# Two gate-and-query projections of layer 1 as seven quarter products each, and a schedule that books the port shared by VectorE and GpSimd

## The chip, the cores and the metric

The kernel runs on one core of a Trainium2 chip. The metric is the time of one launch in microseconds on the device; three runs are given, and one further execution was taken by the hardware profiler.

## The reference, cut to what matters

Two layers on x of 512 tokens x 1024 channels in float32. Layer 0 is a mix of an mLSTM and a sparse attention; layer 1, which the change touches, is a gated linear recurrence with 8 heads of 128:

```python
def hgrn2_layer(h, w_in, b_in, lb, head_norm, w_out):
    proj = h @ w_in + b_in                    # h: 512 x 1024, w_in: 1024 x 4096
    fp, iv, qp, z = jnp.split(proj, 4, axis=-1)
    logf = jnp.log(lb + (1.0 - lb) * jax.nn.sigmoid(fp))
    k = (1.0 - lb) * jax.nn.sigmoid(-fp)
    q = jax.nn.silu(qp)
    o = hgrn2_chunkwise(heads(q), heads(k), heads(iv), heads(logf))
    o = rms_norm(o, head_norm)
    return (o * jax.nn.silu(z)) @ w_out

x = x + layer(rms_norm(x, norm_w))            # for both layers
```

## The kernel before

Every float32 product is made of three float32r products. `cvt_w` splits a weight block of 128 x 1024 into a high part (two ScalarE copies of 512 columns, `whi<-raw`) and a low part (one VectorE subtraction, `wlo<-raw,whi`); activations are split likewise (`h1h`, `h1l`). A matmul triple is then high x high, high weight x low activation, low weight x high activation. Weights come as 512 KB loads on SyncE's queue into 3 buffers `raw` and are split into 4 buffers `whi`, `wlo`, each as soon as the block before in that buffer has been used.

Layer 1's input projection is cut by pairs of heads. `t0` to `t3` give gate and query of two heads each (512 columns: gate and query of one head, then of the other), `r0` to `r3` value and output gate. The order is t0, p0, t1, t2, t3, p1, then the output projections o10 and o11. p0 and p1 are `Pair`: two r projections made at once by Strassen's method, seven products instead of eight, from weight sums in DRAM (`wt`) and activation sums `S1` to `S4` (tiles `ss`). A t projection is a `Group`: 4 blocks of 128 columns, 8 blocks of 128 rows, 3 products, each a matmul that streams 512 tokens past a 128 x 128 weight: 96 matmuls. Its result for a block lies in a PSUM bank (`mx` or `my`); `t_evac` multiplies it by the tokens' norm `rsB` on VectorE and makes from a gate `f` and the key `HB[:, 2]`, from a query `HB[:, 0]` and `HB[:, 1]`.

The recurrence of a head, `hgrn(h)`, takes 7 levels of small matmuls (`sd`, `tq`) and VectorE products on `HB`, then a tail that needs the head's values from p0 or p1. It starts once both heads of a t projection are there, and runs among the next projections' matmuls: heads 0 and 1 in p0, 2 and 3 in t2, 4 and 5 in t3, 6 and 7 in p1, with tails later.

The weight sums are made in layer 0 by GpSimd's own DMA queue from DRAM to DRAM (`AQ.put`): `sums(q, n)` issues step n of eight for pair q, four copies, two accumulations from the weights, and the two steps `t2 += t3` and `t4 += t2` (`wt<-wt`), one step in each of the eight groups nkv to o00, at fixed places of the group's order.

The order of all instructions on every engine is worked out at build time. Generators (`Flow`) emit work in an order of priority; then `Plan.schedule` is a list schedule in which each operation has a price (`price`), begins when its operands, its engine and its buffers are free, and the one with the earliest due time goes first. Six rounds are made and the best by its own clock is kept. Only the order of instructions goes into the program; on the chip each engine runs its own in that order and waits for semaphores. One engine's begin looks at its own clock alone:

```python
def begin(o):
    if o.eng != "T":
        return max(clock[o.eng], o.ready)
```

All instructions have the line of a helper (L407), so rows are told apart by tile names, buffer numbers left out.

Of the kernel before, what the change touches and what calls it, by code (L numbers as in the profile page):

```python
# [28 lines left out]
HBN = 4  # L29
# [7 lines left out]
def _r(a, n):  # L37
# [121 lines left out]
class Op:  # L159
    __slots__ = ("eng", "fn", "a", "k", "cost", "acc", "pred", "succ", "left", "ready", "start", "end", "done", "late", "after",  # L160
                 "load", "cols", "idx", "first", "tiles", "tab", "next")


class Plan:
# [5 lines left out]
    def __init__(self):  # L170
        self.ops, self.hist, self.masks = [], {}, {}
        self.tag, self.order, self.bufs = {}, {}, {}
        self.clock = dict.fromkeys("TVAPQ", 600.0)
        self.xfer, self.table, self.cols = 0.0, 0, [0.0] * 4
        self.born = {}
# [26 lines left out]
    def add(self, eng, fn, a, k, cost):  # L202
# [6 lines left out]
        o.next = None  # L209
        aps = [(x, j == 0) for j, x in enumerate(a) if isinstance(x, bass.AP)]  # L210
# [72 lines left out]
    def schedule(self, pe):  # L283
# [8 lines left out]
        clock, xfer, table, cols = dict(self.clock), self.xfer, self.table, list(self.cols)  # L292

        def begin(o):
            if o.eng != "T":
                return max(clock[o.eng], o.ready)
# [43 lines left out]
        while n_left:  # L340
# [23 lines left out]
            x.end = x.done = clock[e] = t + cost  # L364
            if e == "T":
# [23 lines left out]
        return max(o.done for o in self.ops), (clock, xfer, table, cols)  # L389

    def flush(self, rounds, live=()):
# [10 lines left out]
        (_, (self.clock, self.xfer, self.table, self.cols), when) = best  # L402
# [113 lines left out]
def price(name, fn, a, k):  # L516
# [12 lines left out]
    if k.get("op") == OP.pow:  # L529
        return 300 + 165 * n  # L530
# [4 lines left out]
    return 150 + (2.1 if fn == "tensor_tensor" else 0.86) * n  # L535
# [5 lines left out]
class Paced:  # L541
# [5 lines left out]
    def __getattr__(self, fn):  # L547
        f = getattr(self.eng, fn)

        def go(*a, **k):  # L550
            aps = [x for x in a if isinstance(x, bass.AP)]
            ns = k.pop("_price", None) or price(self.name, fn, a, k)
# [4 lines left out]
            self.plan.add(self.name, f, a, k, ns)  # L557
# [57 lines left out]
def build(tc, I, out):  # L615
# [6 lines left out]
    with ExitStack() as ctx:  # L622
# [258 lines left out]

        def split(name):
# [10 lines left out]
        def rstd(accs, rs, rsB, ev, TPS=TPS, tp_t=tp_t):  # L893
# [7 lines left out]
            P.tensor_tensor(rs, rs, hm[:, :4], op=OP.pow, _price=1950.0)  # L901
# [20 lines left out]
        wt = [dp.tile([128, 8192], F32, name=f"wt{q}", tag=f"wt{q}") for q in range(2)]  # L922
        x1d = dp.tile([128, 8, 512], F32, name="x1d", tag="x1d")
# [5 lines left out]
        def sums(q, n):  # L929
# [4 lines left out]
                     (t1, wblock(b, 0), 1), (t3, wblock(b, 1), 1), (t2, t3, 1), (t4, t2, 1)]  # L934
            AQ.put(*steps[n])
# [10 lines left out]
        with ExitStack() as c0:  # L946
# [738 lines left out]
            def dense0():  # L1685
                for n_, g in enumerate(seq[:-1]):
# [25 lines left out]
        with ExitStack() as c1:  # L1712
# [242 lines left out]

            def t_evac(pr):
                def go(j4, p):
                    hh, j = divmod(j4, 2)
                    h = 2 * pr + hh
                    c = 4 * pr + j4  # L1960
                    t = w_t("tt")
                    V.tensor_tensor(t, p, rsB, op=OP.mult)
                    if j == 0:
                        hbr[0] -= 1
                        assert hbr[0] >= 0
                        HBs[h] = s_t("HB", [128, 3, 512], HBN)
                        fs[h] = s_t("f", [128, 512], HBN)
                        f = fs[h]
                        A.activation(f, t, AF.Sigmoid, bias=pcc("t", c))
                        sg = w_t("sg")  # L1970
                        A.activation(sg, t, AF.Sigmoid, scale=-1.0, bias=ntb[:, c:c + 1])
                        V.tensor_scalar(f, f, oml[:, h:h + 1], lb[:, h:h + 1], op0=OP.mult, op1=OP.add)
                        A.activation(HBs[h][:, 2, :], sg, AF.Copy, scale=oml[:, h:h + 1])
                    else:
                        HB = HBs[h]
                        sq = w_t("sgq")
                        A.activation(sq, t, AF.Sigmoid, bias=pcc("t", c))
                        V.scalar_tensor_tensor(HB[:, 0, :], t, pcc("t", c), sq, op0=OP.add, op1=OP.mult)
# [134 lines left out]
```

## Time and profile before

| | us |
|---|---|
| median of 3 runs | 624.26 |
| lowest and highest of them | 619.97, 624.37 |
| the profiled execution | 622.05 |
| its span, first to last instruction | 620.3 |
| TensorE busy | 610.5 (98%) |
| VectorE busy | 464.6 (75%) |
| ScalarE busy | 326.6 (53%) |
| GpSimd busy | 106.0 (17%) |

PE is TensorE's matmul row, PEld its weight loads, DVE VectorE, ACT ScalarE, POOL GpSimd, SP SyncE; a q behind a name is the engine's queue of instructions that issue or wait. Matmuls overlap and their ends are modelled, so the spacing of their starts says more than their length. x96 behind a name counts instructions; "<-" in brackets names what ended the idle time before.

### The profile page before, as it was taken

The page shows a single profiled execution, that of the slowest core. Times are in us where ns is not written, and L with a number is a line of the kernel's source. Part 1 is how long each engine was busy: PE and PEld are TensorE (multiplying, and loading weights), DVE is VectorE, ACT ScalarE, POOL GpSimd, SP SyncE. Part 2 cuts the span into 40 slices and gives each one's busy share as a digit, 9 for nine tenths or more (in the row PEclk, how much of TensorE's full clock was granted, in tenths as well). Part 3 has the DMA queues.
Part 4 walks back from the last instruction along what each step waited for, and adds up shares of the span by engine and source line. Part 5 has one row for each costly group of instructions (what it writes and reads, how often), then busy time and mean ns, then how long its engine had stood idle before and what let it go on. Part 6 is the DMA issues. An engine that isn't in the chain of part 4 may idle for free.

```text
span 620.3 us, 11687 instructions
## 1 busy us (share of the span) xinstructions
PE 610.5 (98%) x4498; PEld 492.5 (79%) x4498; DVE 464.6 (75%) x979; ACT 326.6 (53%) x778; POOL 106.0 (17%) x140
## 2 busy tenths in 40 slices
PE   8999998999999999999999999999999999999997
PEld 8977886877777777888878887788877877788886
DVE  5878989979888775556555659997588798986441
ACT  6554433676666764373434657456427375565410
POOL 1224351110000010074103110113000100122100
PEclk9998999999999999999999999999999999999999
DMA  8733545625234028048964424374222215473111
GB/s 287 259 139 107 151 133 189 203 70 170 101 71 135 1 42 248 0 122 277 240 209 136 136 89 148 109 230 141 63 77 70 70 32 175 134 281 130 35 69 68
DMA packets 23526, 82.90 MB, mean 134 GB/s; under 512 B 3376, under 2 KB 4272, under 8 KB 20656
## 3 DMA queue, kind: packets, MB, share of 16 engines
q1 hardware_dynamic: 21168, 65.39, 31.9%
q0 software_dynamic: 2304, 16.78, 10.6%
q8 instruction: 35, 0.57, 0.4%
q14 instruction: 19, 0.16, 0.1%
HBM read 77.96 MB, written 20.97 MB: 159 GB/s over the span
## 4 chain that ended last, share of the span: by engine, by line
PE 86%; DVE 6%; DMA 3%; issue 1%; POOL 1%; ACT 1%; SPq 0%; ACTq 0%; DVEq 0%
PE mm L407 30%; PE mx L407 17%; PE my L407 15%; PE sc L407 7%; PE tp L407 5%; PE tq L407 5%; PE ac L407 4%; DMA raw<-in_wall_dram 3%; PE sd L407 2%; DVE wlo L407 1%; POOL krs L407 1%; DVE q L407 1%; DVE x L407 1%; DVE HB L407 1%; DVE ivgg L407 1%
## 5 line engine op out<-in xcount | busy, mean ns | idle before, releaser
L407 ACT ACTIVATE whi<-raw 128x512 fp32r<-128x512 f32 (+1 forms) x184 | 104.9, 614 | 74.7 <-PE my L407 29.3
L407 DVE TENSOR_TENSOR wlo<-raw,whi 128x1024 fp32r<-128x1024 f32 (+1 forms) x96 | 115.3, 1208 | 17.4 <-ACT whi L407 17.2
L407 PE MATMUL mm<-wlo,h0h 128*128 128x512 f32 (+1 forms) x168 | 68.1, 408 | 0.0
L407 PE MATMUL mm<-whi,h0h 128*128 128x512 f32 (+1 forms) x168 | 68.0, 407 | 0.0
L407 PE MATMUL mm<-whi,h0l 128*128 128x512 f32 (+1 forms) x168 | 67.6, 403 | 0.0
L407 ACT ACTIVATE PP<-sc,nm 128x128 f32<-128x128 f32 (+2 forms) x64 | 33.7, 527 | 22.8 <-DVE nm L407 19.4
L407 DVE CUSTOM_DVE_ANT_0 sc<-sc,cz 128x128 f32<-128x128 f32 (+2 forms) x64 | 31.5, 501 | 13.3 <-PE sc L407 10.2
L407 PE MATMUL mm<-h0l,whi 128*128 128x512 f32 x96 | 39.1, 407 | 0.0
L407 PE MATMUL mm<-h0h,whi 128*128 128x512 f32 x96 | 39.0, 406 | 0.1
L407 PE MATMUL mm<-h0h,wlo 128*128 128x512 f32 x96 | 38.1, 396 | 0.4 <-DVE wlo L407 0.4
L407 PEld LDWEIGHTS mm<-whi,h0l 128*128 128x128 f32 x168 | 32.2, 192 | 5.7
L407 PEld LDWEIGHTS mm<-wlo,h0h 128*128 128x128 f32 x168 | 32.2, 192 | 5.7 <-issue 0.2
L407 PEld LDWEIGHTS mm<-whi,h0h 128*128 128x128 f32 x168 | 32.2, 192 | 5.4 <-issue 0.2
L407 DVE TENSOR_TENSOR HB<-HB,tt 128x512 f32<-128x512 f32 x48 | 31.9, 686 | 4.5 <-PE sd L407 3.1
L407 PE MATMUL sc<-kd,q 128*128 128x128 f32 (+3 forms) x128 | 31.8, 333 | 0.0
L407 ACT ACTIVATE PT<-tp 128x384 f32<-128x384 f32 (+1 forms) x48 | 24.1, 526 | 11.0 <-PE tp L407 10.8
L407 POOL TENSOR_TENSOR ivgg<-ivgg,zz 128x256 f32<-128x256 f32 x16 | 17.7, 1106 | 66.0 <-ACT zz L407 66.0
L407 PE MATMUL tp<-cs,PP 128*128 128x128 f32 x160 | 26.7, 276 | 0.0
L407 PEld LDWEIGHTS sc<-kd,q 128*128 128x128 f32 x128 | 22.9, 192 | 4.4 <-ACT PT L407 0.8
L407 PE MATMUL my<-h1l,whi 128*128 128x512 f32 x64 | 25.8, 404 | 0.0
L407 PE MATMUL mx<-h1l,whi 128*128 128x512 f32 x64 | 25.8, 403 | 0.0
L407 PE MATMUL mx<-h1h,whi 128*128 128x512 f32 x64 | 25.7, 402 | 0.0
(374 smaller groups left out, 1535.7 us busy)
## 6 DMA issues: line engine op xcount, KB each, us to landing
raw<-in_wall_dram SPq DMA_DIRECT2D x76, 512.0 KB, 4.1
wt<-in_wall_dram POOLq DMA_DIRECT2D x12, 1024.0 KB, 5.5
raw<-wt SPq DMA_DIRECT2D x16, 512.0 KB, 3.8
wt<-wt POOLq DMA_DIRECT2D x4, 1024.0 KB, 12.6
bias<-in_brow_dram SPq DMA_DIRECT2D x9, 256.0 KB, 4.7
xt<-in_xt_dram SPq DMA_DIRECT2D x8, 256.0 KB, 5.9
w<-in_cw_dram SPq DMA_DIRECT2D x2, 1024.0 KB, 8.8
x<-in_xt_dram SPq DMA_DIRECT2D x2, 1024.0 KB, 9.6
```

Of the source, the lines that this page charges most:

```text
L407: o.fn(*o.a, **k)
```

## The change

Projections t1 and t2 become `Quad`s. Each is seen as a 2 x 2 product of quarters: output columns by head, tokens by halves of 256, rows by halves of 512. Seven products p, each of a 512 x 256 weight quarter (or sum of quarters) and 256 tokens: 2 column blocks x 4 row blocks x 3 split products, 24 matmuls of 256 columns, 168 in all. Products 0, 3, 4, 5 add up in one PSUM bank X, product 1 has a bank Y, 2 and 6 a second Y; the four outputs come from the banks as they stand after products 1, 4, 5 and 6 and from copies of X made by ScalarE after products 0, 3 and 4 (tiles `hold`), added by VectorE. The weights take seven blocks of 512 KB instead of four, each split by `cvt_w`. The weight sums (`wq`) are made in DRAM by `qsums`, eight steps of 512 KB for each of the two projections, issued at four places of a group's order (6, 28, 50, 72) where there were two (10, 60). The host lays the columns of t1 and t2 out by quarters, query ahead of gate. A head's recurrence is handed over after product 5 or 6.

In the list schedule an operation of VectorE or GpSimd may hold a port: all of GpSimd's but memsets (200 ns for a power, else its price), and VectorE's with two inputs in SBUF or plain copies and scalar products from SBUF to SBUF. Such an operation begins no earlier than the port is free. GpSimd's prices are set anew (345 ns + 165 per element for a power, 165 + 2.22 for a product), and the fixed 1950 ns for the power in `rstd` goes.

```diff
+FAST = "t1", "t2"
 G1 = []
 for _p in range(4):
-    G1.append((f"t{_p}", _r(256 * _p, 128) + _r(2048 + 256 * _p, 128)
-               + _r(256 * _p + 128, 128) + _r(2048 + 256 * _p + 128, 128)))
+    _b = [_r(256 * _p, 128), _r(2048 + 256 * _p, 128), _r(256 * _p + 128, 128), _r(2048 + 256 * _p + 128, 128)]
+    G1.append((f"t{_p}", sum([_b[_j ^ (f"t{_p}" in FAST)] for _j in range(4)], [])))
...
-                return max(clock[o.eng], o.ready)
+                return max(clock[o.eng], o.ready, port if o.port else 0.0)
...
+            if x.port:
+                port = t + x.port
...
-        return 300 + 165 * n
+        return 345 + 165 * n
...
-    return 150 + (2.1 if fn == "tensor_tensor" else 0.86) * n
+    return 165 + (2.22 if fn == "tensor_tensor" else 0.86) * n
...
+def port(name, fn, a, k, ns):
+
+    if name not in "VP" or fn == "memset":
+        return 0.0
+    if k.get("op") == OP.pow:
+        return 200.0
+    src = [x for x in (*a[1:], *k.values()) if isinstance(x, bass.AP)]
+    sb = [x for x in src if x.tensor.name[:3] not in PSUMS]
+    big = max(free_size(x) for x in src)
+    two = sum(free_size(x) > 1 or big == 1 for x in sb) > 1
+    fast = fn in ("tensor_scalar", "tensor_copy") and len(sb) == len(src) and a[0].tensor.name[:3] not in PSUMS
+    return ns if name == "P" or two or fast else 0.0
...
+            def convert(self, u):
+                self.fetch(u + RB)
+                self.w[u] = cvt_w(self.raw.pop(u), 512)
+
+            def go(self, nxt=None):
+                X = Y = None
+                for p in range(7):
+                    w = self.w[p]
+                    for c in range(2):
+                        for k in range(4):
+                            first = p < 3 and c + k == 0
+                            yield [w[2]] + self.waits(p) + ([MY if p else MX] if first else [])
+                            if first:
+                                if p:
+                                    Y = my_t()
+                                else:
+                                    X = mx_t()
+                            bank = Y if p in (1, 2, 6) else X
+                            a, o = self.acts(p, k), 256 * k + 128 * c
+                            for x, y in ((0, 0), (1, 0), (0, 1)):
+                                T.matmul(bank[:, 256 * c:256 * c + 256], w[y][:, o:o + 128], a[x],
+                                         start=first and x + y == 0, stop=k == 3 and y == 1, skip_group_check=True)
+                                if y == 0:
+                                    yield ()
+                    fl.cur.t = max(fl.cur.t, fl.pe)
+                    yield from self.evac(p, X, Y)
+                    if p < 3:
+                        self.convert(p + 4)
+                    elif nxt:
+                        nxt.fetch(RB)
+                        nxt.convert(p - 3)
...
-            P.tensor_tensor(rs, rs, hm[:, :4], op=OP.pow, _price=1950.0)
+            P.tensor_tensor(rs, rs, hm[:, :4], op=OP.pow)
...
+        def qsums(name, n):
+            t1, t2, t3, t4 = (wq[name][:, 1024 * i:1024 * (i + 1)] for i in range(4))
+            b11, b12, b21, b22 = (qblock(name, r) for r in range(4))
+            steps = [(t1, b11, 0), (t3, b12, 0), (t2, b11, 0), (t4, b21, 0), (t1, b12, 1), (t3, b22, 1), (t2, t3, 1), (t4, t2, 1)]
             AQ.put(*steps[n])
...
-                        if 2 <= n_ < 10 and i in (10, 60):
-                            sums(i // 60, n_ - 2)
+                        if 2 <= n_ < 10 and i % 22 == 6 and i < 88:
+                            a = i // 22
+                            if a < 2:
+                                sums(a, n_ - 2)
+                            else:
+                                qsums(FAST[a - 2], n_ - 2)
...
+            def q_evac(pr):
+                b = {}
+
+                def go(p, X, Y):
+                    h = 2 * pr + (p in (3, 4, 6))
+                    X, Y = (x and cut(x, (2, 256)) for x in (X, Y))
+                    if p in (0, 3, 4):
+                        b[p] = w_t("hold", (2, 256))
+                        A.activation(b[p], X, AF.Copy, scale=-1.0 if p else 1.0)
+                    if p in (1, 4):
+                        yield [ev1[1], lambda: hbr[0] > 0]
+                        heads_t(h)
+                    s0 = 256 * (p in (4, 5))
+                    rb = cust(rsB, [[0, 2], [1, 256]], s0)
+                    if p in (1, 4, 6):
+                        t = b[{1: 0, 4: 4, 6: 3}[p]]
+                        V.tensor_tensor(t, Y, t, op=OP.add)
+                    if p in (0, 2, 3):
+                        return
+                    HB = HBs[h]
+                    V.tensor_tensor(HB[:, :2, s0:s0 + 256], X if p == 5 else t, rb, op=OP.mult)
+                    if p > 4:
+                        gate(h, HB[:, 1, :])
+                        query(h, HB[:, 0, :])
+                        V.tensor_tensor(HB[:, 1, :], HB[:, 0, :], fs[h], op=OP.mult)
+                        fl.add(hgrn(h), 1 + h)
...
+            def quad(pr):
+                n = f"t{pr}"
+
+                def src(u):
+                    b, c = ((0, 0), (0, 2), (1, 0), (1, 1), (1, 2), (1, 3), (0, 3))[u]
+                    return wq[n][:, 1024 * c:1024 * c + 1024] if b else qblock(n, c)
+
+                def acts(p, k):
+                    if p in (0, 1, 5):
+                        k4, o = ((0, 0), (1, 0), None, None, None, (1, 256))[p]
+                        return [h1[k4][x][:, k, o:o + 256] for x in range(2)]
+                    t = SS[("S1", "S2", "S3", None, "S4")[p - 2]]
+                    return [t[:, x, k, :] for x in range(2)]
+
+                def waits(p):
+                    return [] if p in (0, 1, 5) else [E1(("S1", "S2", "S3", None, "S4")[p - 2])]
+                return Quad(n, src, acts, waits, q_evac(pr))
...
+                elif n in FAST:
+                    gs.append(quad(pr))
```

`heads_t`, `gate` and `query` are the old code of `t_evac`, split into functions; `t_evac` keeps t0 and t3.

## Rows read from the trace of the kernel before

**Rows 1.** Busy time of the engines, part 1 of the page (share of span, instructions).

```profile
PE 610.5 (98%) x4498; PEld 492.5 (79%) x4498; DVE 464.6 (75%) x979; ACT 326.6 (53%) x778; POOL 106.0 (17%) x140
```

**Rows 2.** Stages: window, us, busy PE, PEld, DVE, ACT, POOL (instructions), clock, DMA share, GB/s.

```profile
0.00:349.60 349.60, 344.51 (x1851) 277.38 (x1852) 263.01 (x609) 190.51 (x454) 70.95 (x96) 1.00 0.49 148
...
374.40:420.90 46.50, 46.25 (x543) 36.20 (x543) 44.68 (x69) 25.81 (x52) 6.91 (x7) 1.00 0.54 168
420.90:448.70 27.80, 27.56 (x144) 23.02 (x144) 18.31 (x43) 15.89 (x44) 5.20 (x7) 1.00 0.27 83
448.70:480.60 31.90, 31.50 (x539) 24.15 (x538) 27.64 (x57) 16.39 (x39) 1.58 (x3) 1.00 0.26 81
480.60:514.40 33.80, 33.60 (x479) 27.06 (x477) 27.93 (x64) 18.70 (x55) 3.40 (x6) 1.00 0.21 64
514.40:561.20 46.80, 46.80 (x518) 36.46 (x517) 42.40 (x71) 26.63 (x61) 8.53 (x9) 1.00 0.57 196
```

**Rows 3.** Pieces of the chain of waits: start us, us, what (count).

```profile
327.67 22.07 PE mm L407 x96
...
613.99 2.85 PE mx L407 x24
```

**Rows 4.** Matmuls of the last group (start us, us) and a group of weight loads.

```profile
607.51 0.28 PE L407 MATMUL my<-y1h,whi 128*128 128x256 f32 x1
607.63 0.28 PE L407 MATMUL my<-y1l,whi 128*128 128x256 f32 x1
...
L407 PEld LDWEIGHTS mx<-y1h,wlo 128*128 128x128 f32 x40 | 7.5, 189 | 1.2
```

**Rows 5.** Groups: whole span, then two in t2: busy us, mean ns | idle before.

```profile
L407 DVE TENSOR_TENSOR wlo<-raw,whi 128x1024 fp32r<-128x1024 f32 x88 | 111.7, 1275 | 16.2 <-ACT whi L407 16.0
L407 ACT ACTIVATE whi<-raw 128x512 fp32r<-128x512 f32 x176 | 101.7, 622 | 73.3 <-PE my L407 29.3 <-PE mm L407 15.3 <-DMA raw<-in_wall_dram 11.8
...
L407 DVE TENSOR_TENSOR wlo<-raw,whi 128x1024 fp32r<-128x1024 f32 x5 | 6.1, 1220 | 1.3 <-ACT whi L407 1.3
L407 DVE TENSOR_TENSOR tt<-my,rsB 128x512 f32<-128x512 f32 x2 | 1.4, 692 | 1.4 <-PE my L407 1.4
```

**Rows 6.** Timeline at 296.4 to 298.4: transposes and the copy that waits for them.

```profile
296.57 0.60 PE L407 MATMUL tp<-cs,nd 128*128 128x128 f32 x4
...
297.20 0.60 ACT L407 ACTIVATE ymh<-tp 128x512 fp32r<-128x512 f32 x1 [0.90 <-PE tp L407]
```

**Rows 7.** A load in the chain, then the timeline of ScalarE and TensorE behind it.

```profile
300.81 13.24 DMA raw<-in_wall_dram
...
314.15 1.15 ACT L407 ACTIVATE whi<-raw 128x512 fp32r<-128x512 f32 x2 [4.44 <-DMA raw<-in_wall_dram]
315.21 0.58 ACT L407 ACTIVATE ymh<-tp 128x512 fp32r<-128x512 f32 x1
...
315.84 0.50 PE L407 MATMUL mm<-ymh,whi 128*128 128x512 f32 x1 [1.20 <-ACT ymh L407]
```

**Rows 8.** DMA: queue 0 from 280 to 325 us; issues of whole span; GpSimd issuing.

```profile
q0 software_dynamic: 576, 4.19, 44.9%
...
raw<-in_wall_dram SPq DMA_DIRECT2D x76, 512.0 KB, 4.1
...
wt<-wt POOLq DMA_DIRECT2D x4, 1024.0 KB, 12.6
...
L407 POOL DMA_DIRECT2D wt<-in_wall_dram x12 | 8.4, 729 | 0.8 <-issue 0.6
```

**Rows 9.** Timeline: VectorE at 63.41, GpSimd from 78.44.

```profile
63.41 2.31 DVE L407 TENSOR_TENSOR wlo<-raw,whi 128x1024 fp32r<-128x1024 f32 x1
...
78.44 2.04 POOL L407 TENSOR_TENSOR krs<-krs,hm 128x4 f32<-128x4 f32 x1
...
81.89 1.01 POOL L407 TENSOR_TENSOR krs<-krs,hm 128x4 f32<-128x4 f32 x1
```

More of the change, by code (lines that the diff above doesn't have):

```diff
@@ L160 @@
     __slots__ = ("eng", "fn", "a", "k", "cost", "acc", "pred", "succ", "left", "ready", "start", "end", "done", "late", "after",
-                 "load", "cols", "idx", "first", "tiles", "tab", "next")
+                 "load", "cols", "port", "idx", "first", "tiles", "tab", "next")
 class Plan:
@@ L173, in __init__ @@
         self.clock = dict.fromkeys("TVAPQ", 600.0)
-        self.xfer, self.table, self.cols = 0.0, 0, [0.0] * 4
+        self.xfer, self.table, self.cols, self.port = 0.0, 0, [0.0] * 4, 0.0
         self.born = {}
@@ L209, in add @@
         o.next = None
+        o.port = k.pop("_port", 0.0)
         aps = [(x, j == 0) for j, x in enumerate(a) if isinstance(x, bass.AP)]
@@ L291, in schedule @@
         self.latest(target)
-        clock, xfer, table, cols = dict(self.clock), self.xfer, self.table, list(self.cols)
+        clock, xfer, table, cols, port = dict(self.clock), self.xfer, self.table, list(self.cols), self.port
         def begin(o):
             if o.eng != "T":
-                return max(clock[o.eng], o.ready)
+                return max(clock[o.eng], o.ready, port if o.port else 0.0)
             t = max(clock["T"], part if len(o.cols) == 4 else 0.0, o.ready)
@@ L388, in schedule @@
                         offer(q)
-        return max(o.done for o in self.ops), (clock, xfer, table, cols)
+        return max(o.done for o in self.ops), (clock, xfer, table, cols, port)
     def flush(self, rounds, live=()):
@@ L401, in flush @@
             pe = sorted(pe, key=lambda o: o.start)
-        (_, (self.clock, self.xfer, self.table, self.cols), when) = best
+        (_, (self.clock, self.xfer, self.table, self.cols, self.port), when) = best
         for o, w in zip(self.ops, when):
@@ L551, in go @@
             aps = [x for x in a if isinstance(x, bass.AP)]
-            ns = k.pop("_price", None) or price(self.name, fn, a, k)
+            ns = price(self.name, fn, a, k)
             self.flow.work(self.name, ns)
@@ L556, in go @@
                     self.flow.last[x.tensor.name] = self.flow.cur.t
-            self.plan.add(self.name, f, a, k, ns)
+            self.plan.add(self.name, f, a, dict(k, _port=port(self.name, fn, a, k, ns)), ns)
         return go
@@ L880, in go, with __init__, fetch @@
                             nxt.convert(u - 14)
+        class Quad:
+            def __init__(self, name, src, acts, waits, evac):
+                self.name, self.src, self.acts, self.waits, self.evac = name, src, acts, waits, evac
+                self.w, self.raw = {}, {}
+            def fetch(self, n):
+                for u in range(min(n, 7)):
+                    if u not in self.raw and u not in self.w:
+                        raw = wp.tile([128, 1024], F32, name="raw", tag="raw", bufs=RB)
+                        self.raw[u] = raw, dma(raw, self.src(u), 4)
+            def convert(self, u):
[28 more added lines that the diff above has]
+                        nxt.convert(p - 3)
         def split(name):
@@ L1963, in go @@
                     if j == 0:
[L1964 to L1972, printed above, removed]
@@ L2066, in pack @@
         + [tile_w(e_out[:, :512]), tile_w(e_out[:, 512:])]
-        + [tile_w(wo[:, c]) for _, c in G1]
+        + [quarters(tile_w(wo[:, c])) if n in FAST else tile_w(wo[:, c]) for n, c in G1]
         + [tile_w(o_out[:, :512]), tile_w(o_out[:, 512:])], axis=1)
```

37 lines of the change are left out of this document (30 added, 7 removed).

## The prediction

> **What bounds it now.** Read the busy shares first: TensorE is busy 610.5 of 620.3 us and VectorE 464.6 [rows 1]. A busy TensorE only says that few holes are left, so next comes the table by stage, cut at the borders of layer 1's projections [rows 2]: p0, t1, t2, t3 and p1. In each of them TensorE is busy to within 0.4 us of the stage's length at a granted clock of 1.00. VectorE is the second engine, and unevenly: 44.68 of 46.50 us in p0, 18.31 of 27.80 in t1, 27.64 of 31.90 in t2, 27.93 of 33.80 in t3. So a stage lasts as long as its matmuls unless VectorE needs longer, and p0 stands at that edge already; of the two stages that change, t2 is nearer to it. The length of a matmul is not its busy time (matmuls overlap) but the spacing in an unbroken run, which the chain of work shows: 96 matmuls of 512 columns in 22.07 us, 229.9 ns each, and 24 of 256 columns in 2.85 us, 118.8 ns each [rows 3].
>
> **Term 1, the matmuls.** A projection of one pair of heads had 4 column blocks x 8 row blocks x 3 split products = 96 matmuls of 512 columns: 96 x 229.9 ns = 22.07 us. The quad has 7 products x 2 column blocks x 4 row blocks x 3 = 168 of 256 columns: 168 x 118.8 ns = 19.95 us. Saved: 2.12 us each, 4.24 us for t1 and t2. The last group of the kernel before is of the very form that comes (a new 128x128 weight for every 256 columns), so this price is measured, not scaled: starts lie 0.12 us apart [rows 4].
>
> A weight load takes 0.189 us on its own row [rows 4], more than that spacing, and yet it is hidden. The Trainium skill (TensorE: Matmul & The Clock Gate, Part 3, The mechanism) says the opposite, that a load overlaps running matmuls only where the row group differs, and gives a load of 128 columns as 128/1.2 = 107 ns; by that, an estimate from the page, the 72 added loads would cost 7.7 us a projection less the 2.6 us that 1/8 fewer columns save. The trace disagrees: all loads here are of full rows and 0.12 us apart. The rule stays as rival E.
>
> **Term 2, the bank turns.** Product 3 is added into bank X, ScalarE copies X out, and only then may product 4 write X; the same between 4 and 5. The one-bank turn is put together from rows: a 256-column matmul shows 0.28 us where the next could have started after 0.12, so 0.16 of drain [rows 4]; 0.03 from TensorE's end (296.57 + 0.60) to ScalarE's start and 0.60 for a 512-column copy out of PSUM [rows 6]; 0.05 from ScalarE's end (315.21 + 0.58) back to TensorE [rows 7]. That is 0.84 us, four times. Queued in front on ScalarE there can be a half conversion of 0.62 [rows 5], so at most 1.46 x 4 = 5.8 us; at least 0, if recurrence matmuls of other heads fill each hole. In t1 little else is there to run (27.80 - 22.07 = 5.7 us of tails), in t2 9.8 us: I take t1's two as bare (1.7) and 0.3 for t2's: +2.0 us. Queued behind the waiting matmul stands all of TensorE's order, the recurrence of the other heads too, so a hole is filled only by what the schedule put there. Product 6 cannot fill them: it adds to bank Y, which VectorE must have read after product 4.
>
> **Term 3, VectorE and ScalarE.** Seven weight blocks instead of four: per quad 3 more low-part subtractions of 1.22 us and 6 more half conversions of 0.62. Folding the products together adds 3 VectorE additions, priced as the 512-column product out of PSUM, 0.69, [rows 5] and 3 ScalarE copies of 0.60 [rows 6]. The four products by `rsB`, the gates and the queries keep their number and size; the host's new column order leaves every load at 512 KB. VectorE +5.7 us, ScalarE +5.5 us per quad. ScalarE stays below 22 of its 30 us. VectorE: t1 18.3 + 5.7 = 24.0 in about 27.4, covered. t2 27.6 + 5.7 = 33.4 in about 30.1: 3.3 us too much. What slips is the level work of heads 2 and 3, into t3, where VectorE has 33.80 - 27.93 = 5.9 us free; p0 shows TensorE keeping pace with VectorE at 96% [rows 2]. Bounds 0 and +3.3; I take +0.5, nearer the lower end for p0's sake. The 3 more loads of 512 KB per quad meet a DMA share of 0.27 and 0.26 and cost nothing; without that cover the 4.1 us that such a load takes [rows 8] would be exposed once.
>
> **Term 4, the sums in DRAM.** Sixteen transfers of 512 KB join the sixteen of 1 MB on GpSimd's queue in layer 0. Their issue is 16 x 0.73 = 11.7 us of GpSimd [rows 8], which there is busy 70.95 of 349.60 us [rows 2]: covered; a reciprocal root queued behind an issue comes up to 0.73 later. The last step of each sum waits on GpSimd for the step before it to land; behind it stands only the adding up of squares for layer 1's norm. The transfers are another matter at one place. Between 280 and 325 us four accumulating DRAM-to-DRAM transfers hold 44.9% of all 16 engines, 20.2 us for 4 MB, hence 2.5 us of all engines per 512 KB [rows 8]. A weight load issued at 300.81 took 13.24 us; ScalarE, in order, stood 4.44 us on it with the copy `ymh` behind it, and TensorE stood 1.20 us for `ymh` [rows 7]. The change puts four more accumulations of 512 KB next to them: 10.1 us of all engines. Upper bound: all of it ahead of that load, +10.1 us. Lower: the new order puts `ymh` ahead of the conversion, -1.2. The extra transfers queue mostly behind the old ones of the same queue, so the load shares with as busy a neighbour as before: I take +0.3. The Trainium skill (DMA: Bandwidth & Descriptors, Anatomy of one DMA) would price a 512 KB transfer of this queue at 2.0 us and bytes over 436 GB/s, 3.2 us, an estimate; 1 MB accumulations measured 12.6 here against 4.4 by the page, so I go by the row.
>
> **Term 5, the booked port.** The schedule only orders instructions; the chip overlaps what it likes. What there is to win: a low-part subtraction that met a GpSimd power took 2.31 us at 63.41, not 1.22, and a power 2.04, not 1.01 [rows 9]. The mean of all 88 is 1275 ns against 1220 in t2, so 88 x 0.055 = 4.8 us of VectorE [rows 5]. That is the bound of a gain if all of it held up TensorE, and I take the same as the bound of a loss, since a new order of every engine can also expose waits. TensorE is idle 9.8 us in all, and VectorE mostly has slack: -0.5.
>
> **Sum.** -4.2 + 2.0 + 0.5 + 0.3 - 0.5 = -1.9 us. The profiled execution took 622.05 us: 620.3 of span and 1.75 around it. That gives **620.2 us**. The median of the three runs shown is 624.26, the lowest 619.97, so the profiled one lies between; the forecast is 0.65% under the median.
>
> **Rivals.**
> A, the sum above, 616 to 624: chance 0.54. That the booking moves nothing that matters (GpSimd is busy 1.58 to 8.53 us a stage in layer 1) is part of it: 620.7.
> B, all holes filled: recurrence work of heads 2 and 3, handed over one product (2.85 us) earlier, covers the bank turns, VectorE fits, and the booking brings half its bound. -4.2 - 2.4 = -6.6: 615.4. For it: t1's idle VectorE. Against: no head is ready when t1's turns come. 0.20.
> C, VectorE sets t2's pace and conversions stand before every copy: -4.2 + 5.8 + 3.3 + 0.3 - 0.5 = +4.7: 626.8. For it: t2's 33.4 in 30.1. Against: p0. 0.13.
> D, slower: the added accumulations run ahead of o01's first weights, and TensorE waits for `ymh` 10.1 us longer: -1.9 - 0.3 + 10.1 = +7.9: 630.0. It decides once that load lands over 8 us later than 314.05. For it: that queue alone holds 44.9% of the engines there. Against: transfers of one queue take turns with the load's. 0.10.
> E, slower: loads bound the 256-column matmuls at 0.189 us: 168 x 0.189 = 31.8 against 22.07 us, +19.4 for both, with the other terms +2.3: 643.8. It is the rule named under term 1; rows 3 and 4 speak against it. 0.03.
>
> **Numbers.** Adding all lower bounds gives -10.2 (612), all upper ones +19.8 (642). Eight in ten: 613 to 629, which takes in A, C and most of B, and leaves D half and E out; A alone is 616 to 624. One per cent is about what a measurement of this kernel can tell from no change (the three runs spread 0.7%). Against 624.26, faster by over 1% means below 618.0: most of B and A's lowest part, 0.23. Slower means above 630.5: half of D, E and C's top, 0.10. Within 1%: 0.67.
>
> **What would show it.** Unbroken runs of quad matmuls at 2.85 us per 24 (term 1; at 4.5, E). Holes of about 0.8 us ended by ScalarE's copy of X, in t1 (term 2). VectorE above 95% in t2 and heads 2 and 3 later in t3 (term 3). The first o01 weights landing near 314 and the wait for `ymh` (term 4; D if near 324). Subtractions above 2 us gone (term 5). I am wrong if a whole stage beyond t1 and t2 moves by over 3 us, for the new order is worked out for all of both layers.

## The result, and the profile after

The changed kernel takes 630.87 us (median of six runs, 628.57 to 634.17) against 622.47 us for the kernel before on the same chip: a ratio of 1.0145, interval 1.0113 to 1.0178. The forecast was 620.2 us, its range 613 to 629. The change makes the kernel slower by 1.45%. The profiled executions behind the traces took 632.98 and 622.05 us; they lie 10.9 us apart where the medians lie 8.4, so the traces tell where the time went and the ratios how much.

The page of the changed kernel answers [rows 1]; the second line is the queue of the sums over the whole span, the third line is the chain of waits by engine, in which DMA had 3% before.

```profile
PE 612.5 (97%) x4642; PEld 498.4 (79%) x4642; DVE 470.0 (75%) x991; ACT 336.6 (53%) x796; POOL 110.5 (18%) x156
...
q0 software_dynamic: 4608, 25.17, 16.2%
...
PE 79%; DMA 9%; DVE 6%; ACT 3%; issue 2%; SPq 0%; POOL 0%; ACTq 0%; DVEq 0%
```

TensorE's busy time hardly moved, while the span grew by 10.5 us (620.3 to 630.8). The table by stage, cut where layer 1's projections begin, says where; columns as in [rows 2].

```profile
0.00:359.20 359.20, 347.55 (x1850) 279.04 (x1851) 259.80 (x609) 190.51 (x454) 75.92 (x112) 0.98 0.57 167
...
384.60:431.80 47.20, 47.20 (x544) 36.30 (x543) 44.42 (x70) 26.61 (x58) 6.07 (x8) 1.00 0.50 155
431.80:459.05 27.25, 26.30 (x218) 25.48 (x217) 19.84 (x34) 16.18 (x43) 4.84 (x6) 1.00 0.49 155
459.05:485.98 26.93, 26.91 (x524) 24.84 (x524) 24.90 (x41) 16.39 (x33) 0.99 (x2) 1.00 0.49 151
485.98:521.00 35.02, 35.02 (x510) 27.57 (x510) 32.44 (x77) 22.66 (x58) 3.49 (x6) 1.00 0.21 61
521.00:570.30 49.30, 47.87 (x568) 36.45 (x567) 45.18 (x87) 28.54 (x69) 8.77 (x8) 1.00 0.56 187
```

Set against [rows 2]: layer 0 lasts 359.2 us instead of 349.6, +9.6. That is nearly the whole loss, in a layer whose matmuls the change does not touch. In layer 1, t1 and t2 together take 54.2 us instead of 59.7, t3 35.0 instead of 33.8, p1 49.3 instead of 46.8. The quads do shorten their own stages, but the others give it back: t0 and p0 are 0.6 and 0.7 us longer, the output projections 1.4 us (60.5 instead of 59.1), so that layer 1 as a whole lasts 271.6 us instead of 270.7.

In layer 0 the loss sits at two places. At each, ScalarE waits for a late load with a conversion, the result that TensorE needs stands behind it in ScalarE's order, and TensorE stops. The first place, on ScalarE and TensorE (start us, us, what, idle before):

```profile
245.67 1.15 ACT L411 ACTIVATE whi<-raw 128x512 fp32r<-128x512 f32 x2 [5.81 <-DMA raw<-in_wall_dram]
246.72 1.12 ACT L411 ACTIVATE E<-sc,apr 128x128 f32<-128x128 f32 x4
...
244.51 0.39 PE L411 MATMUL mm<-whi,h0l 128*128 128x512 f32 x1
247.90 0.79 PE L411 MATMUL sc<-nM,selr 36*128 36x512 f32 x1 [3.00 <-ACT E L411]
```

The second place is that of [rows 7], where TensorE waited 1.20 us before:

```profile
321.43 1.15 ACT L411 ACTIVATE whi<-raw 128x512 fp32r<-128x512 f32 x2 [4.40 <-DMA raw<-in_wall_dram]
322.49 0.58 ACT L411 ACTIVATE ymh<-tp 128x512 fp32r<-128x512 f32 x1
...
319.27 0.39 PE L411 MATMUL ac<-yn,wlo 128*128 128x512 f32 x1
323.12 0.79 PE L411 MATMUL mm<-ymh,whi 128*128 128x512 f32 x1 [3.46 <-ACT ymh L411]
```

The chain of waits names the two loads (start us, us):

```profile
234.60 10.98 DMA raw<-in_wall_dram
...
305.84 15.49 DMA raw<-in_wall_dram
```

Each can be set against the same load in the kernel before, which took 7.1 us at the first place (issued at 234.84) and 13.24 us at the second (issued at 300.81, [rows 7]). They take 3.9 and 2.3 us longer, and TensorE waits 3.0 and 2.3 us longer.

Around the end of each stop TensorE is granted half its clock, 1.2 instead of 2.4 GHz, for 6.8 us (window, us, then as in [rows 2]; the clock is the third number from the end):

```profile
247.00:253.85 6.85, 5.95 (x23) 5.21 (x23) 3.89 (x6) 1.99 (x8) 0.00 (x0) 0.50 0.76 258
253.85:260.00 6.15, 6.15 (x38) 4.74 (x38) 3.79 (x9) 2.04 (x8) 0.00 (x0) 1.00 0.00 0
...
322.10:328.95 6.85, 5.83 (x13) 4.33 (x14) 1.82 (x2) 2.06 (x4) 0.00 (x0) 0.50 1.03 254
```

TensorE counts as busy there, but does half the work. What each place cost is read from two matmuls that stand just ahead of the two places in both kernels. In the kernel before:

```profile
241.57 0.49 PE L407 MATMUL sc<-nM,selr 36*128 36x512 f32 x1
...
314.25 0.39 PE L407 MATMUL ac<-yn,wlo 128*128 128x512 f32 x1
```

and in the changed kernel the first of them

```profile
240.89 0.49 PE L411 MATMUL sc<-nM,selr 36*128 36x512 f32 x1
```

and the second at 319.27, above. The changed kernel is 0.7 us ahead at the first and 5.0 us behind at the second, so the first place cost 5.7 us: 3.0 of waiting, the other 2.7 at half clock. From there to layer 1 the lag grows to 9.6, so the second place cost 4.6: 3.46 - 1.20 = 2.3 of more waiting, and 2.3 at half clock. About half of the loss is waiting, half is the clock behind it.

### The profile page after: what moved, and what is told of

It reads as the page before. It is cut to its first block, busy times and chain, and to the rows that moved or that the text cites. A ratio compares the mean times of both kernels' runs of the same rounds, so it can differ in the third digit from the quotient of the medians.

```text
span 630.8 us, 12047 instructions
## 1 busy us (share of the span) xinstructions
PE 612.5 (97%) x4642; PEld 498.4 (79%) x4642; DVE 470.0 (75%) x991; ACT 336.6 (53%) x796; POOL 110.5 (18%) x156
## 4 chain that ended last, share of the span: by engine, by line
PE 79%; DMA 9%; DVE 6%; ACT 3%; issue 2%; SPq 0%; POOL 0%; ACTq 0%; DVEq 0%
PE mm L411 30%; PE mx L411 15%; PE my L411 12%; PE sc L411 7%; DMA raw<-in_wall_dram 7%; PE tp L411 5%; PE tq L411 4%; PE ac L411 4%; DVE wlo L411 2%; PE sd L411 2%; DMA raw<-wt 2%; ACT whi L411 1%; DVE HB L411 1%; DMA raw<-wqt 1%; DVE ivgg L411 1%
## 5 line engine op out<-in xcount | busy, mean ns | idle before, releaser
L411 ACT ACTIVATE whi<-raw 128x512 fp32r<-128x512 f32 (+1 forms) x196 | 111.7, 615 | 92.0 <-DMA raw<-in_wall_dram 31.7
L411 DVE TENSOR_TENSOR wlo<-raw,whi 128x1024 fp32r<-128x1024 f32 (+1 forms) x102 | 119.3, 1178 | 31.6 <-ACT whi L411 31.2
L411 DVE TENSOR_TENSOR HB<-HB,tt 128x512 f32<-128x512 f32 x48 | 33.3, 708 | 3.1 <-PE sd L411 1.6
L411 PEld LDWEIGHTS tp<-cs,PP 128*128 128x128 f32 x160 | 20.5, 140 | 5.5 <-issue 0.9
L411 PE MATMUL mx<-h1h,whi 128*128 128x512 f32 (+1 forms) x64 | 22.5, 351 | 0.4 <-ACT whi L411 0.2
L411 PE MATMUL mx<-h1h,wlo 128*128 128x512 f32 (+1 forms) x64 | 22.1, 346 | 0.0
## 6 DMA issues: line engine op xcount, KB each, us to landing
wt<-wt POOLq DMA_DIRECT2D x4, 1024.0 KB, 18.6
```

The costliest lines, as they stand in the source:

```text
L411: o.fn(*o.a, **k)
```

## The experiments

Theory T: the sixteen added sums crowd the DMA engines, weight loads come late, ScalarE in its order passes the delay to TensorE, and the half clock about doubles it. Theory P: the booked port and the new prices give layer 0 a worse order. Ratios are to the kernel before, run beside each group of kernels on one chip.

**The change without the added sums.**

```diff
-    return wq[n][:, 1024 * c:1024 * c + 1024] if b else qblock(n, c)
+    return qblock(n, c)
...
-                            else:
-                                qsums(FAST[a - 2], n_ - 2)
```

> The changed kernel without the sixteen quarter-sum transfers: its quads read plain quarters of the weights where they read sums, so two projections come out with other values; loads, products, conversions and orders of work are otherwise those of the change. Theory T (the added sums crowd the DMA engines in layer 0, weight loads come late, ScalarE in order holds up TensorE, which then runs at half clock): layer 1 starts near 350 us instead of 359.2, the two stretches of half clock at 247 and 322 us are gone, and the total is 621 (618 to 624). Theory P (the booked port and the new prices give layer 0 an order that is 9 us worse): layer 1 still starts near 359 and the total stays at 630. Either way layer 1 itself keeps its 267.8 us.

Measured: 623.31 us, ratio 1.0006 (0.9983 to 1.0029); in the profiled execution, the longest of ten, layer 1 starts at 352.9 us and lasts 269.9 to the end of the span. The wait for `E` is gone, and its load lands 7.5 us after issue, against 7.1 before. A wait for `ymh` remains, with 6.8 us of half clock from 316.2 us on, against my expectation that both stretches would go (TensorE, then ScalarE):

```profile
315.26 0.49 PE L411 MATMUL mm<-ymh,whi 128*128 128x512 f32 x1 [2.34 <-ACT ymh L411]
...
311.87 1.33 ACT L411 ACTIVATE whi<-raw,pcs 128x512 fp32r<-128x512 f32 x2 [9.30 <-DMA raw<-in_wall_dram]
```

So T holds for the total and for the first place: the added sums are worth 1.4% (1.0145 to 1.0006), some 8 us. For the second place it is not shown: without the added sums the two loads there still land 15.9 and 13.9 us after issue, beside the old 1 MB sums, which here stand at the changed places.

**The added sums in the kernel before**, unread, at the changed places:

```diff
-                        if 2 <= n_ < 10 and i in (10, 60):
-                            sums(i // 60, n_ - 2)
+                        if 2 <= n_ < 10 and i % 22 == 6 and i < 88:
+                            a = i // 22
+                            if a < 2:
+                                sums(a, n_ - 2)
+                            else:
+                                qsums(("t1", "t2")[a - 2], n_ - 2)
```

> The kernel before with only the DMA work of the change: the sixteen quarter-sum transfers are issued at the changed places (and the eight steps of each old sum too), nobody reads them; prices, port and projections are the old ones. Theory T: layer 1 starts 6 to 10 us later than the 349.6 us of before, with weight loads of 12 to 15 us near 240 and 315 to 330, total 628 to 632. Theory P: no change, 621 to 624.

Measured: 630.78 us, ratio 1.0133 (1.0084 to 1.0182), the loss of the whole change. Its profiled execution, the shortest of the four (span 625.7 us), starts layer 1 at 354.2, 4.6 us later than before where T expected 6 to 10, and has the first wait clearly and the second weakly:

```profile
246.29 0.49 PE L407 MATMUL sc<-nM,selr 36*128 36x512 f32 x1 [2.13 <-ACT E L407]
...
318.89 0.51 PE L407 MATMUL mm<-ymh,whi 128*128 128x512 f32 x1 [1.55 <-ACT ymh L407]
```

No quad, no booked port, no new price is in this kernel: the transfers alone, the added ones and the old ones at the changed places, cost 1.3%, some 8 us.

**The change without its planner part**, and **the planner part alone.** The first removes these lines from the change, the second adds them to the kernel before (with what carries `port` through the schedule):

```diff
-            self.plan.add(self.name, f, a, k, ns)
+            self.plan.add(self.name, f, a, dict(k, _port=port(self.name, fn, a, k, ns)), ns)
...
-        return 300 + 165 * n
+        return 345 + 165 * n
...
-    return 150 + (2.1 if fn == "tensor_tensor" else 0.86) * n
+    return 165 + (2.22 if fn == "tensor_tensor" else 0.86) * n
```

> The change without its planner part: quads and quarter sums as changed, the port not booked and the old prices. Theory T: the loss stays, layer 1 starts near 358, total 627 to 632. Theory P: layer 0 is back at 350 and the total is 620 to 623.

> The kernel before with only the planner part: port booked, new prices, no quads and no added sums. Theory T: within 2 us of before, 620 to 624. Theory P: layer 1 starts near 359, total 630 to 633.

Measured: without it 627.33 us, ratio 1.0069 (1.0035 to 1.0104); alone 622.30 us, ratio 1.0004 (0.9988 to 1.0021). P falls as the whole cause: the planner part alone does nothing to the time, and without it a loss remains. But by the ratios only about half of the loss (0.69 of 1.45%) remains, so beside the sums the planner part seems to add to it. The profiled execution without it, the longest of its ten, starts layer 1 at 358.1 and has both waits (2.16 and 4.10 us). The stages of the planner part alone (layer 0; t1 to t3; p1) show layer 0 1.7 us shorter than in [rows 2], t1 to t3 0.4 us shorter than their 93.5, p1 0.75 us shorter than its 46.8; the stages not shown give that back, t0 and p0 among them, which take 25.5 and 47.2 us here and 25.4 and 47.2 in the changed kernel, but 24.8 and 46.5 before and 24.9 and 46.5 in the change without the planner part:

```profile
0.00:347.90 347.90, 343.74 (x1850) 276.99 (x1851) 259.94 (x609) 189.69 (x454) 66.43 (x96) 1.00 0.50 148
...
420.55:513.60 93.05, 92.01 (x1160) 74.04 (x1159) 72.71 (x158) 49.03 (x131) 8.90 (x15) 1.00 0.27 80
513.60:559.65 46.05, 45.87 (x512) 35.72 (x511) 42.19 (x70) 26.24 (x61) 5.53 (x7) 1.00 0.58 195
```

Two stretches, cut at the matmuls that priced the two places above, put these versions side by side (us in the profiled executions; the first from that `sc<-nM,selr` to that `ac<-yn,wlo`, the second from there to layer 1):

| version | first | second |
|---|---|---|
| the kernel before | 72.7 | 35.3 |
| the changed kernel | 78.4 | 39.9 |
| the change without the added sums | 72.6 | 40.3 |
| the added sums in the kernel before | 76.8 | 37.2 |
| the change without its planner part | 76.8 | 40.1 |
| the planner part alone | 72.9 | 34.1 |

The first stretch is long in each version with the added sums at the changed places, and in no other. The second is long in every version with quads and the changed places, with the added sums or without; in the old order the same transfers cost 1.9 us there.

**Other places for the same transfers: three that fail.** In a table of places, (group, unit) to (sum, step), replacing the `if` above, the thirty-two steps were put as early as can be:

```diff
+for _s in range(8):
+    for _a in range(4):
+        _n, _i = ((_s, 6 + 22 * _a), (6, 2 + 6 * _a), (6, 28 + 6 * _a))[max(0, _s - 5)]
+        PLACES.setdefault((_n, _i), []).append((_a, _s))
```

> The changed kernel with all thirty-two sum transfers kept, only issued earlier: steps 0 to 4 one group sooner or more, steps 5 to 7 ahead of the long stretch between 197 and 228 us in which GpSimd used to wait, so that none is left near 235 or after 280. Theory T: weight loads at 235 to 251 and 300 to 335 take 4 to 6 us again, TensorE's waits of 3.2 us for E and 3.6 us for ymh go, no half clock there, layer 1 starts at 350 to 353, total 620 to 624; loads may be late before 225 instead, as 25 MB of sums need 126 us of all engines. A rival (the bytes cost the same wherever they go): layer 1 still near 357 to 360 and total 628 to 631, with holes before 225.

Measured: 636.87 us, ratio 1.0235 (1.0204 to 1.0265), layer 1 from 367.0 on. The two old waits are gone (no wait above 0.41 us between 240 and 350), but step 0 now runs beside the program's first loads:

```profile
14.61 0.85 PE L417 MATMUL sc<-whi,h0h 128*128 128x288 f32 x2 [7.38 <-ACT whi L417]
```

and its first window, as in [rows 2]:

```profile
0.00:60.00 60.00, 46.62 (x289) 41.41 (x289) 31.90 (x71) 25.54 (x44) 11.35 (x26) 0.86 0.78 273
```

The kernel before was busy 58.22 us in this first window, at 0.97. Both expected totals were too low, mine (620 to 624) and the rival's (628 to 631): the cost moved to a place where the loads are waited for at once, and grew. I had overlooked that place.

The second variant moved p1's sum into layer 1 and kept the early start; the third did the same in the kernel before:

```diff
+LATER = {("t0", 20): 0, ("t0", 70): 1, ("p0", 30): 2, ("p0", 70): 3, ("p0", 110): 4, ("p0", 150): 5, ("t1", 50): 6, ("t2", 50): 7}
...
+                        if (a.name, i) in LATER:
+                            sums(1, LATER[a.name, i])
```

> As f1_sums_early, but the sum of 8 MB that only the last projection pair reads is issued in layer 1 (two steps in t0, four in p0, one each in t1 and t2), so layer 0 carries the 16.8 MB it carried before. Theory T: layer 1 starts at 348 to 350.5, layer 1 keeps its 266 to 268, total 616 to 619.5, below the kernel before by 0.4 to 1%. Rival: the moved transfers delay layer 1's loads and total is 622 or more.

> The kernel before, without quads or port, with its two sums placed as in f2_wide_sum_later (8 MB early in layer 0, 8 MB in layer 1). It says what the places alone bring: Theory T: the 1.4 us wait for ymh at 316 goes, total 618 to 621; the quads' own worth is then f2 less f3, expected -1 to -2 us.

Measured: 642.01 us, ratio 1.0319 (1.0286 to 1.0353), and 636.46 us, ratio 1.0225 (1.0201 to 1.0249). Both wait at the start as the first variant did (one wait of 6.42 us at 15.70, one of 4.59 at 12.25), and p0 takes 52.5 and 54.1 us instead of 46.5, with waits of TensorE for `whi` there (2.12 us at 417.60, 3.75 at 411.01). p0 had no room for these transfers; the rival holds for the place I chose.

**Places between the crowds.** Step 0 where the change has it, steps 1 to 6 sooner (all issued by 205 us), step 7 near 270 us:

```diff
+        _n, _i = ((2, 6 * _a), (2, 48 + 12 * _a), (3, 6 + 22 * _a), (4, 6 + 22 * _a), (5, 6 + 22 * _a),
+                  (6, 2 + 6 * _a), (6, 28 + 6 * _a), (7, 66 + 6 * _a))[_s]
```

> The changed kernel with all thirty-two sum transfers in layer 0 and between the two crowded ends: step 0 where the change has it (about 55 us), the others sooner, steps 5 and 6 ahead of the long GpSimd wait at 197 us, step 7 near 270 us; none with the first loads of the program (which cost f1_sums_early 13 us of waits before 60 us) and none after 285. Theory T: no waits for E at 247 and for ymh at 322, no half clock there; weight loads between 60 and 120 us may be late by a few us; layer 1 starts at 349 to 353, total 619 to 624. If the bytes cost the same wherever they go: layer 1 at 357 or later, total over 628.

> g1_sums_between with the old prices and no booked port. Against g1 it tells what the planner part does once the transfers are out of the way: with no interplay both agree within 2 us (619 to 624); if the booked order itself is worse for the quads, g2 is 2 to 4 us below g1, as e3_quads_no_port was below the changed kernel.

> The kernel before, with its own sixteen sum transfers at the places of g1_sums_between, no quads, no port. What the places are worth alone: Theory T says the 1.4 us wait for ymh near 316 goes, total 619.5 to 622; the quads' own worth is g1 or g2 less this.

Measured side by side: the whole change with these places 621.08 us, ratio 0.9982 (0.9965 to 0.9998); without the planner part 625.04 us, 1.0047 (1.0020 to 1.0074); the kernel before with these places 623.87 us, 1.0023 (1.0005 to 1.0041). The first is the only version that beats the kernel before, by 0.2%, with all 25 MB of sums in it. The stages of its profiled execution, the shortest of ten (layer 0; t1 and t2; t3; p1):

```profile
0.00:347.50 347.50, 343.31 (x1850) 275.54 (x1851) 259.07 (x609) 190.71 (x454) 81.82 (x112) 1.00 0.60 173
...
420.00:474.35 54.35, 53.34 (x740) 50.44 (x739) 44.87 (x75) 32.97 (x76) 5.83 (x8) 1.00 0.50 153
474.35:509.30 34.95, 34.95 (x510) 27.58 (x510) 32.32 (x77) 22.52 (x58) 3.51 (x6) 1.00 0.21 58
509.30:556.75 47.45, 47.45 (x568) 36.60 (x567) 45.58 (x89) 28.71 (x69) 8.77 (x8) 1.00 0.59 196
```

Layer 0 is 2.1 us shorter than before, of which the planner part alone brings 1.7, although its DMA share rose from 0.49 to 0.60: what counts is where the bytes lie. The places alone brought the kernel before no gain but 0.2% of loss (I had expected a small gain; TensorE waits 2.00 us at 295.0 there for `nd`, a product of VectorE). Change less places is 621.08 - 623.87 = -2.8 us: what quads and port are worth together once the sums are out of the way. The profiled executions of these two lie 4.1 us apart (617.8 and 621.9 us of span); of that 2.8 lie in layer 0, which has no quads (347.5 and 350.3 us), and only 1.3 in layer 1. The planner part, worth nothing alone, brings 4.0 us here, more than I had allowed for and the other way than at the changed places, where it costs some 4.7 (ratios 1.0145 with and 1.0069 without it, from two groups of runs). Why the sign turns was not settled.

**The same transfers, and a schedule that knows of them.** At the changed places, one line tells the schedule that a sum holds the DMA engines; the line can move any instruction, and what it moved is read from the trace:

```diff
                 x.done = x.end + x.k["_ns"]
+                xfer = max(xfer, x.end) + (0.24 if "accum_op" in x.k else 0.28) * (x.k["_ns"] - 2000.0)
```

> The changed kernel, its sums at the places of the change; the schedule is only told that a sum holds the DMA engines (about 5 us for each added 1 MB, 2.9 us for each copied one, half for quarters), so a weight load behind sums is planned late. In ScalarE's order this puts the last two copies ymh ahead of the conversions whi that waited for late loads at 315 to 328 us; the conversion ahead of E at 247 stays where it was. Theory T with ScalarE's order as its second link: loads stay as late as before (12 to 15 us near 300 to 335), yet TensorE's 3.6 us wait for ymh shrinks below 1.5 us, and its half clock at 322 goes; the wait for E at 247 stays; layer 1 starts at 353 to 356, total 624 to 627. Rival (TensorE needs the late weights themselves, order or not): wait and total stay, 629 to 632.

Measured: 624.52 us, ratio 1.0051 (1.0029 to 1.0073); the profiled execution, the shortest of five, starts layer 1 at 349.2. Between 285 and 336 us the loads are as late as in the changed kernel (median 11.2 us after issue against 10.6), but `ymh` stands between the halves of the conversion instead of behind a later one. TensorE waits for it nowhere. First the loads (issues: count, KB, median us to landing), then the timeline of ScalarE and TensorE:

```profile
raw<-in_wall_dram SPq DMA_DIRECT2D x8, 512.0 KB, 11.2
```

```profile
311.70 0.72 ACT L412 ACTIVATE whi<-raw,pcs 128x512 fp32r<-128x512 f32 x1 [4.00 <-DMA raw<-in_wall_dram]
312.33 0.58 ACT L412 ACTIVATE ymh<-tp 128x512 fp32r<-128x512 f32 x1
...
246.94 0.50 PE L412 MATMUL sc<-nM,selr 36*128 36x512 f32 x1 [2.23 <-ACT E L412]
```

The wait for `E`, whose order did not change, stayed, and the first stretch takes 75.1 us. The second takes 33.4 us, as in the three versions with the places between. So at the second place late loads cost time only through the order of the instructions behind them: the second link of T is shown there.

**Only the first crowd removed:**

```diff
+        _n, _i = (6, 2 + 6 * _a) if _s == 4 else (6, 28 + 6 * _a) if _s == 5 else (_s + 2, 6 + 22 * _a)
```

> The mirror image: of the change only steps 4 and 5 of all sums are issued sooner, ahead of the long GpSimd wait at 197 us, so that no four of them are let go together at 228; steps 6 and 7 stay in the crowded stretch after 285. Theory T: the 3.2 us wait for E at 247 and the half clock behind it go, the wait for ymh and its half clock stay; layer 1 starts at 353 to 356, total 624 to 627. Each crowd is then worth about half of the loss.

Measured: 629.46 us, above the expected 624 to 627, ratio 1.0135 (1.0102 to 1.0168), layer 1 from 356.8 on. The wait for `E` is gone (the first stretch takes 72.6 us) and that for `ymh` stays, as expected, but a new wait stands where the sums went; each of the two has 3.4 us of half clock:

```profile
198.18 0.61 PE L417 MATMUL sc<-kd,q 128*128 128x384 f32 x2 [2.30 <-ACT PP L417]
...
321.94 0.80 PE L417 MATMUL mm<-ymh,whi 128*128 128x512 f32 x1 [3.46 <-ACT ymh L417]
```

That each crowd is half of the loss is therefore not shown.

## Why the prediction was wrong, point by point

**What bounds the kernel**: right; wherever TensorE did not stand, it set the pace.

**Term 1, right.** Unbroken runs of quad matmuls show the 2.85 us per 24 of [rows 3], so rival E is out:

```profile
483.35 2.86 PE my L411 x24
```

The section of the Trainium skill that term 1 cites (TensorE: Matmul & The Clock Gate, Part 3, The mechanism) says more than term 1 took from it: a load into the background weight buffer, too, is pulled ahead of running matmuls. That would allow what these runs show, so page and trace need not disagree; which kind a load here is, no run shows.

**Term 2, +2.0, too high.** Of the 0.84 us of a turn at most 0.2 us shows as a wait. In t1 the schedule filled the turns with matmuls of other heads (`tq`) and with t2's first product, a possibility that term 2 did not see: 20 of its 24 matmuls (told by their operands `h1h` and `h1l` and the bank `mx`) stand between t1's products 3 and 4, and wait 0.21 us for their own weight conversion; the last four stand between products 4 and 5, ahead of a wait of 0.21 us for the copy `hold`. In t2 64 small `sd` matmuls fill a turn:

```profile
443.27 1.50 PE L411 MATMUL tq<-ivgg,kT 128*128 128x128 f32 x12
444.98 0.39 PE L411 MATMUL mx<-h1h,whi 128*128 128x256 f32 x1 [0.21 <-ACT whi L411]
...
451.50 0.50 PE L411 MATMUL mx<-ss,whi 128*128 128x256 f32 x2
...
456.18 0.38 PE L411 MATMUL mx<-h1h,whi 128*128 128x256 f32 x1 [0.21 <-ACT hold L411]
...
478.66 0.74 PE L411 MATMUL sd<-HB 128*32 128x16 f32 x64
```

What rival B said of t1, that waiting work fills the turns, is nearer than "bare".

**Term 3, +0.5, the right direction.** VectorE is at 24.90 of 26.93 us in t2, not above 95%, and at 32.44 of 35.02 in t3, where it was 27.93 of 33.80: the level work slipped, as said, and t3 became 1.2 us longer. Terms 1 to 3 together were to bring -1.7 us in t1 to t3; they brought 93.5 - 89.2 = 4.3, and p1 gave back 0.65 us (in the version with the places between) to 2.5 us (in the changed kernel, of which TensorE waits 1.44 us once for a conversion whose load took over 10 us, with no sum beside it). Over the whole of layer 1 the gain is 0.7 to 2.0 us: with the planner part 272.3 us without quads against 271.6 (the changed kernel) and 270.3 (places between), without it 270.7 against 270.0 and 269.3. The -1.7 is right for the layer, but not for the stages that it was worked out for.

**Term 4 is the step that failed: +0.3 forecast, +9.6 measured in layer 0 of the profiled execution.** Three things in it were wrong. First, "the extra transfers queue mostly behind the old ones of the same queue, so the load shares with as busy a neighbour as before". The queue of the sums now carries 6.29 MB between 285 and 336 us, and the median load there lands 10.6 us after issue (between 280 and 325 us of the kernel before: 4.5); two 1 MB loads of `x` on the weights' own queue take 20.1 us instead of 9.6 (issues: count, KB, median us to landing):

```profile
q0 software_dynamic: 1152, 6.29, 61.9%
...
raw<-in_wall_dram SPq DMA_DIRECT2D x8, 512.0 KB, 10.6
wt<-wt POOLq DMA_DIRECT2D x4, 1024.0 KB, 18.6
...
wqt<-wqt POOLq DMA_DIRECT2D x4, 512.0 KB, 19.7
```

The load I watched, issued at 300.81 and landed at 314.05, is issued at 305.84 in the changed kernel and lands at 321.33. Of these 7.3 us, 5.0 are the lag from the first place. The other 2.3 are its longer flight (15.49 instead of 13.24 us), and by as much TensorE waits longer; these 2.3 us stand against the +0.3. Rival D's condition ("over 8 us later") was just missed, and the 10.1 us that it priced did not come. Nor is it shown that the added sums alone set the cost of this place, as the second stretch is as long without them.

Second, I looked at one place. GpSimd waits at 197 us for a buffer until 227.8 us; before, two issues stood behind that wait, after the change four, let go together at 228.0 to 229.6 us just ahead of the weight loads. That the places went from two to four a group stands in the diff; the queue behind that wait was not counted. It cost 5.7 us, the larger part, and this part is shown to be the added sums' work.

Third, a wait of TensorE was priced at its own length. The half clock behind it cost about as much again.

The Trainium skill (DMA: Bandwidth & Descriptors, Queues, rings and completion order) says that each engine takes turns between its queues, a packet at a time. With packets of equal length, a load with a sum beside it would by this rule take about twice its time, an estimate. In the version with only the first crowd removed the load of the first place, issued at 239.26 us with no sum beside it, landed after 3.4 us; in the changed kernel, issued at 234.60, it landed after 11.0, over three times as long. But the packets were not equally long. Between 228 and 252 us of the changed kernel (queue 0 has the sums, queue 1 the loads):

```profile
q0 software_dynamic: 576, 3.15, 70.0%
q1 hardware_dynamic: 692, 2.28, 24.4%
```

Of 16 engines' 24 us, a packet of the sums took 0.47 us and one of the loads 0.14. If these are the packets that the rule means, which no run shows, one of each in turn makes a load up to 4.5 times as long, an estimate; so the measured factor does not speak against the rule.

**Term 5, -0.5, about right as a lone term.** Alone the booking brings nothing (1.0004), though low-part subtractions fall from 1208 to 1178 ns over all 96 (96 x 0.030 = 2.9 us of VectorE; before, then with the planner part alone):

```profile
L407 DVE TENSOR_TENSOR wlo<-raw,whi 128x1024 fp32r<-128x1024 f32 (+1 forms) x96 | 115.3, 1208 | 17.4 <-ACT whi L407 17.2
L410 DVE TENSOR_TENSOR wlo<-raw,whi 128x1024 fp32r<-128x1024 f32 (+1 forms) x96 | 111.9, 1178 | 23.7 <-ACT whi L410 23.7
```

Its effect is not a term that can be added, though: it was 4.0 us one way with the places between and some 4.7 the other way at the changed places, both within the bound of 4.8. [rows 9] was misread in one point: what GpSimd ran beside the subtraction at 63.41 us was a product (`qk`, from 63.34 on, 1.29 us); the power before it ended at 63.36. And of two subtractions above 2 us one stayed (2.27 us at 360.40 in the changed kernel).

Rival C did not come. D, at 0.10, had the right kind of mechanism, a late load ahead of `ymh` on ScalarE, and got too small a chance. That its 630.0 lies so near the measured 630.87 is luck: it put 10.1 us of waiting at the second place, where 2.3 us came, and had neither the first place nor the half clock.

## What to carry to other kernels

A transfer off the critical path is priced by what waits in order behind the loads that it delays: take each load in the stretch, the instruction that waits for it, and what stands behind that instruction on its engine, and look for a wait that lets queued issues go together. The same bytes cost 9 us, or 15, or nothing, by where they were put, and one line that told the schedule of the busy DMA engines gave back 6 us without moving a byte. Price a stop of TensorE of some microseconds above its length when the clock rows show half clock behind such stops. A gain in the stages that a change touches can be given back in those around it: add up the whole layer.

## What the runs showed of the hardware

The stops of 3.00 and 3.46 us in the changed kernel each came with 6.8 us at 1.2 GHz; stops of 2.30 and 3.46 us in the version with only the first crowd removed with 3.4 us each; the 2.23 us stop in the version with the told schedule with none, its mean granted clock being 0.999. So the price of a stop varied between its own length and about twice that. Accumulating DRAM-to-DRAM transfers of 512 KB landed 19.7 us after issue (median) beside others of their queue and the weight loads, about as late as those of 1 MB (18.6): in this crowd their size did not tell.
